# A streaming encoder trunk: joins and closing additions of the last MLP halves by VectorE in place of accumulating DMA

## The chip, the cores and the metric

The kernel runs on one core of a Trainium2 chip. A core has TensorE for matmuls (PE in the profile), VectorE (DVE), ScalarE (ACT), GpSimd (POOL) and SyncE (SP), each with an in-order queue of its own, and 16 DMA engines. The metric is the device time of one execution in microseconds (us); what counts is the median of several runs. Line numbers (L564) are those of the kernel before. In the changed kernel everything below L564 stands four lines lower.

## The reference

The input is 256 tokens by 2048 channels in float32. Two layers are computed, the first with a convolution module as token mixer, the second with latent attention; each is followed by an MLP, and one norm ends the whole:

```python
for layer in range(DEPTH):
    h = rms_norm(x, norm_mixer_g[layer])
    x = x + (conv_module(h, ...) if layer % 2 == 0 else mla(h, ...))
    h = rms_norm(x, norm_mlp_g[layer])
    x = x + jnp.square(jax.nn.relu(h @ mlp_w1[layer])) @ mlp_w2[layer]
return rms_norm(x, final_norm_g)
```

The change concerns the last line in the loop: the product of a 256 x 8192 matrix with the 8192 x 2048 weights mlp_w2, and its addition to the residual x.

## The kernel before

**Arithmetic.** The residual lies in SBUF as one tile, xs, of 128 partitions x 2 token blocks (t) x 2048 columns, in float32. A float32 weight matrix comes in 1 MB pieces (raw, three buffers). Each piece is split into an upper part hi by ScalarE (L169, or L487 in the mixed form) and the rest lo by VectorE (L173, or L488); hi and lo have six buffers each (WB = 6), one half of a piece in each. A product is then three matmuls, hi x hi, hi x lo and lo x hi (mm3, L202 to L204).

**The MLP.** It runs in two halves of the 8192 inner channels (hf = 0, 1). In a half, the first product fills the inner activations, eight groups of 512 channels, and the second product adds the half's share to xs. The second product goes over the output columns in pairs of 512-column blocks, n = 0 and n = 2, so xs is touched by two pairs in each half. Within a pair an object of the class Sums holds eight PSUM banks. Part of the channel groups are *plain*: four banks e collect them directly, one bank per token block and column block. The others are *mixed*: seven products in place of eight on quarter matrices, formed from sums of weights (L495 to L497, VectorE) and of activations; four further banks, u1, u6, u7 and u5, collect some of the seven, the rest go into the banks e. So a unit of two channel blocks of 128 (a *quad* where it is mixed) costs VectorE two 1024-column splits if it is plain, and seven instructions if it is mixed. In the last half there are three mixed groups (layer 0 and layer 1: `MIXED[layer, 1] = (0, 2, 4)`) and five plain ones. For n = 0 units of the two kinds alternate. For n = 2 the last half uses product_A, whose plain pieces have four channel blocks of one column block; mixed quads are put between them in the numbers 1, 2, 1, 2 (the function `between`), and the block n = 3 follows, with plain groups only.

**Joins and closing additions.** When all mixed quads of a pair are done, `join` (L566) turns u1, u6, u7 and u5 into four sums: ScalarE copies u1 into a tile a (L570), VectorE adds the others (L571 to L574), and each of the four results, in SBUF tiles v, goes to its place in xs by `put` (L563): a DMA of 128 x 512 float32 that adds to its destination, issued by GpSimd (L564). When the plain units are done too, `close` (L578) adds the banks e: those of the first column block by VectorE directly (L584), those of the second by a ScalarE copy into a tile v (L587) and another accumulating DMA. The last half of a layer calls join for n = 0 and n = 2 and close for n = 0 only; the banks e of n = 2 and 3 are added by product_A's `add` on VectorE (L377).

**Who reads xs next.** In the last half each finished block is prepared for the following norm (`prepare`): ScalarE squares it and sums the squares (L400, reading xs), and in layer 0 TensorE turns it (L266). In layer 1 VectorE multiplies it by the final gain (L1787).

**The order.** Outside the parts under `manual_schedule` a scheduler sets each engine's order when the kernel is built, and a wait is placed wherever an instruction reads or writes what another one has touched. An instruction that waits holds up all that stands behind it in its engine's queue.

Of the kernel before, what the change touches and what calls it, by code (L numbers as in the profile page):

```python
# [15 lines left out]
ALU = mybir.AluOpType  # L16
# [9 lines left out]
NNB = D // NB  # L26
# [52 lines left out]
def trunk_kernel(  # L79
# [26 lines left out]
    nc = tc.nc  # L106
# [37 lines left out]
    def acc_tile():  # L144
        return psum["acc"].tile([P, NB], F32, tag="acc", name=nm("acc"))
# [375 lines left out]
    class Sums:  # L521


        def __init__(self, n):
            self.n = n
            ps = [acc_tile() for _ in range(8)]
            e, self.u = (ps[:4], ps[4:])[:: 1 if n == 0 else -1]
            self.e = [e[2 * t : 2 * t + 2] for t in range(T)]
            self.begun = set()
# [31 lines left out]
            return xs[:, t, (self.n + c) * NB : (self.n + c + 1) * NB]  # L561

        def put(self, t, c, o):  # L563
            nc.gpsimd.dma_start(self.place(t, c), o, accum_op=ALU.add)  # L564

        def join(self, room):  # L566

            u1, u6, u7, u5 = self.u
            a, b, c, d = (room() for _ in range(4))
            nc.scalar.activation(a, u1, AF.Copy)  # L570
            nc.vector.tensor_tensor(b, u6, a, op=ALU.add)  # L571
            nc.vector.tensor_tensor(c, u7, b, op=ALU.add)
            nc.vector.tensor_tensor(d, u5, c, op=ALU.add)
            nc.vector.tensor_tensor(b, u5, b, op=ALU.add)  # L574
            for (t, n), o in (((0, 0), a), ((1, 0), c), ((1, 1), d), ((0, 1), b)):
                self.put(t, n, o)

        def close(self, room):  # L578

            for c in range(2):  # L580
                for t in range(T):
                    e, x = self.e[t][c], self.place(t, c)
                    if c == 0:
                        nc.vector.tensor_tensor(x, e, x, op=ALU.add)  # L584
                    else:
                        o = room()
                        nc.scalar.activation(o, e, AF.Copy)  # L587
                        self.put(t, c, o)

    def mlp(layer, ssq, next_gain, finish=None, before=None, beside=None, after_up=None):  # L590

        with ExitStack() as cx:
# [22 lines left out]
            for hf in range(HALVES):  # L615
                last = hf == HALVES - 1
# [3 lines left out]
                for g in range(ng):  # L620
# [26 lines left out]
                    for b2 in range(2):  # L647
                        v = v_tile()
                        for b in range(2):
                            o = ps[2 * b2 + b]  # L650
# [18 lines left out]
                def mixed_quad(sums, i):  # L669
                    g, b = ms[i]  # L670
                    sums.mixed(w, k_lo + 4 * g + 2 * b, gs[g][0][:, b], gs[g][1][:, b], i == len(ms) - 1)

                for n in range(0, NNB - 2 * last, 2):
                    sums = Sums(n)
                    ks = [4 * g + 2 * b for g in plain for b in range(2)]
                    at, head = 0, HEAD[n // 2]
                    for i, k in enumerate(ks):
                        upto = -(-len(ms) * (i - head + 1) // (len(ks) - head - TAIL + 1))
                        while at < min(upto, len(ms)):
                            mixed_quad(sums, at)  # L680
                            at += 1
                        if i == len(ks) - TAIL + 1:
                            sums.join(room)
                        sums.plain(w, k_lo + k, hi, lo, k, i == len(ks) - 1)
                    sums.close(room)
                    if last:
                        due += [n, n + 1]
                if last:
                    sums = Sums(NNB - 2)
                    n2 = NNB - 2  # L690

                    def between(n, u, due):
                        if n == n2 and u < len(plain) - 1:
                            for i in range(*(len(ms) * max(i, 0) // (len(plain) - 1) for i in (u, u + 1))):
                                mixed_quad(sums, i)
                        if n == n2 and u == len(plain) - 1:
                            sums.join(room)

                    if after_up is not None:
                        after_up()  # L700
                    product_A(
                        w, k_lo, nkh, hi, lo, add, prepare, range(n2, NNB), due,
                        finish=(lambda t: finish(nssq, t)) if finish is not None else None,
                        before=lambda: before(nssq),
                        groups=plain, banks={n2 + c: [sums.e[t][c] for t in range(T)] for c in range(2)},
                        begun=sums.begun, beside=between,
                    )
# [3 lines left out]
    with ExitStack() as cx:  # L711
# [235 lines left out]
        with tc.manual_schedule():  # L947
# [100 lines left out]
            upper_x, lower_x, last = ((0, 0),), ((0, 1),), ((1, 0),)  # L1048
# [48 lines left out]
            for c in range(1, KC + 1):  # L1097
                n = UC * c
# [6 lines left out]
                if c == KC:  # L1105
# [8 lines left out]
                    c = KC - 1  # L1114
# [105 lines left out]
            for m in range(NP):  # L1220
# [25 lines left out]
                for q in {NP - 3: (0, 1, 4), NP - 2: (5, 2, 3), NP - 1: (6, 7)}.get(m, ()):  # L1246
                    t, i = divmod(q, NNB)
# [13 lines left out]
    def rotary_tables(pool):  # L1261
# [54 lines left out]
        nc.scalar.activation(cos, an2, AF.Sin)  # L1316

    ssq = mlp(0, ssq, g_mix[1], beside=rotary_tables)
    repool("a", acc=6, tr=2)


    with ExitStack() as cx:
# [321 lines left out]
        with tc.manual_schedule():  # L1644
# [87 lines left out]
            for g in range(NG):  # L1732
                for i in range(HG):
                    h = g * HG + i

                    n = -(-len(work) // (HG - i))
# [41 lines left out]
    with ExitStack():  # L1778
# [10 lines left out]
        def finish(ssq, t):  # L1789

            n = NNB - 1
            if t == T - 1:

                nc.vector.tensor_scalar(
                    part[t], ssq[:, t, n : n + 1], scalar1=1.0 / D, scalar2=part[t], op0=ALU.mult, op1=ALU.add
                )
                n += 1
            v = small.tile([P, 1], F32, tag="msf", name=nm("ms"))
            w = small.tile([P, 1], F32, tag="wsf", name=nm("ws"))
            y = small.tile([P, 1], F32, tag="ysf", name=nm("ys"))  # L1800
            q = small.tile([P, 1], F32, tag="qsf", name=nm("qs"))
            nc.scalar.activation(w, ssq[:, t, n : n + 1], AF.Sqrt, scale=1.0 / D, bias=part[t])
            nc.vector.tensor_scalar(v, ssq[:, t, n : n + 1], scalar1=1.0 / D, scalar2=part[t], op0=ALU.mult, op1=ALU.add)
            refined(w, v, y, q)

            stores = []
            cuts = [0, NB // 2, NB, 2 * NB, 3 * NB, D]
            for i, (c0, c1) in enumerate(zip(cuts, cuts[1:])):
                ob = xs[:, t, c0:c1]
                if c1 == D:  # L1810
                    nc.vector.scalar_tensor_tensor(
                        out=ob, in0=ob, scalar=y, in1=gfs[0][:, c0:c1], op0=ALU.mult, op1=ALU.mult
                    )
                elif i in (1, 3):
                    nc.scalar.activation(ob, ob, AF.Copy, scale=y)
                else:
                    nc.vector.tensor_scalar(ob, ob, scalar1=y, scalar2=None, op0=ALU.mult)
                dst = out[0, t * P : (t + 1) * P, c0:c1]
                if i in (1, 3) and t == T - 1:
                    stores.append((dst, ob))  # L1820
                else:
                    nc.sync.dma_start(dst, ob)

            for dst, ob in stores:
                nc.scalar.dma_start(dst, ob)
# [3 lines left out]
        def before(ssq):  # L1829

            for t in range(T):
                m = small.tile([P, 1], F32, tag="msp", name=nm("msp"))
                nc.vector.tensor_reduce(m, ssq[:, t, : NNB - 1], axis=AX.X, op=ALU.add)
                nc.vector.tensor_scalar(m, m, scalar1=1.0 / D, scalar2=EPS, op0=ALU.mult, op1=ALU.add)
                part.append(m)
                for n in range(NNB - 1):
                    gained(t, n)

        mlp(1, ssq, None, finish, before, after_up=load_gf)


# [24 lines left out]
```

## Time and profile before

| what | value |
|---|---|
| median of 3 runs | 1954.84 us (1952.97 to 1958.66) |
| the profiled execution | 1957.43 us, its span 1954.8 us |
| TensorE matmuls / VectorE / ScalarE / GpSimd busy | 99% / 80% / 55% / 13% of the span |
| accumulating DMAs of L564 | 44, each 256 KB |
| granted TensorE clock, mean | 0.999 |
| last half of layer 0: its first pair ends, its second pair's join | about 902 us, about 960 us |
| last half of layer 1: its first pair ends, its second pair's join | about 1857 us, about 1915 us |

The span is the profiled execution from its first to its last instruction; the time around it is a little longer. Views of the trace: the *waits* give who waited for whom, in us in total, number of times and longest; the *stretches* give for each window its length, the engine's busy time, in brackets the number of instructions, the granted clock (1.00 is full), the share of the DMA engines in use and GB/s; the *timeline* gives start, duration, engine, line, operation, written and read tiles, and in square brackets the idle time before the instruction and what ended it.

### The profile page before, as it was taken

The page shows a single profiled execution, that of the slowest core. Times are in us where ns is not written, and L with a number is a line of the kernel's source. Part 1 is how long each engine was busy: PE and PEld are TensorE (multiplying, and loading weights), DVE is VectorE, ACT ScalarE, POOL GpSimd, SP SyncE. Part 2 cuts the span into 40 slices and gives each one's busy share as a digit, 9 for nine tenths or more (in the row PEclk, how much of TensorE's full clock was granted, in tenths as well). Part 3 has the DMA queues.
Part 4 walks back from the last instruction along what each step waited for, and adds up shares of the span by engine and source line. Part 5 has one row for each costly group of instructions (what it writes and reads, how often), then busy time and mean ns, then how long its engine had stood idle before and what let it go on. Part 6 is the DMA issues. An engine that isn't in the chain of part 4 may idle for free.

```text
span 1954.8 us, 28567 instructions
## 1 busy us (share of the span) xinstructions
PE 1929.8 (99%) x10823; PEld 1688.8 (86%) x10823; DVE 1557.0 (80%) x2404; ACT 1084.2 (55%) x1616; POOL 259.2 (13%) x216
## 2 busy tenths in 40 slices
PE   9999999999999999999999999999999999999998
PEld 8999888888888888887789998888888888888876
DVE  7999988877999677697866766877789976777886
ACT  5667755554555455454566565555555655555554
POOL 6999100000010000001001310000000010000000
PEclk9999999999999999999999999999999999999999
DMA  7665556664586766467765445466647686665755
GB/s 232 208 193 174 169 180 212 194 187 158 194 250 227 236 191 194 151 215 205 220 194 146 135 138 192 157 210 194 192 153 232 212 277 188 190 193 194 232 170 169
DMA packets 222569, 379.15 MB, mean 194 GB/s; under 512 B 16216, under 2 KB 91232, under 8 KB 222176
## 3 DMA queue, kind: packets, MB, share of 16 engines
q1 hardware_dynamic: 214768, 363.28, 58.6%
q0 software_dynamic: 6336, 11.54, 3.3%
q10 hardware_dynamic: 1328, 2.52, 0.4%
q8 instruction: 84, 1.38, 0.3%
q14 instruction: 53, 0.43, 0.1%
HBM read 363.68 MB, written 2.10 MB: 187 GB/s over the span
## 4 chain that ended last, share of the span: by engine, by line
issue 25%; PE 19%; DVE 2%; DMA 2%; ACT 1%; POOL 1%; DVEq 0%; ACTq 0%; POOLq 0%
PE acc L633 6%; PE acc L634 3%; PE acc L204 3%; PE acc L202 3%; PE acc L203 3%; DMA xs<-v 2%; DVE lo L488 1%; POOL xs L564 1%; DVE lo L173 1%; DVE raw L495 0%; DMA raw<-in_mlp_w 0%; PE acc L1623 0%; ACT hi L487 0%; ACT hi L169 0%; PE tr L1614 0%
## 5 line engine op out<-in xcount | busy, mean ns | idle before, releaser
L173 DVE TENSOR_TENSOR lo<-raw,hi 128x1024 fp32r<-128x1024 f32 (+2 forms) x519 | 618.9, 1206 | 282.7 <-ACT hi L169 275.6
L169 ACT ACTIVATE hi<-raw 128x1024 fp32r<-128x1024 f32 (+2 forms) x584 | 596.8, 1039 | 397.4 <-PE acc L633 216.3
L633 PE MATMUL acc<-xt,hi 128*128 128x512 f32 x2048 | 710.5, 391 | 0.0
L634 PE MATMUL acc<-xt,lo 128*128 128x256 f32 x2048 | 577.9, 282 | 0.0
L633 PEld LDWEIGHTS acc<-xt,hi 128*128 128x128 f32 x2048 | 384.5, 188 | 79.5
L634 PEld LDWEIGHTS acc<-xt,lo 128*128 128x128 f32 x2048 | 388.1, 189 | 0.2
L487 ACT ACTIVATE hi<-raw 128x1024 fp32r<-128x1024 f32 x224 | 206.6, 948 | 201.0 <-DVE raw L495 118.4
L488 DVE TENSOR_TENSOR lo<-raw,hi 128x1024 fp32r<-128x1024 f32 x224 | 239.0, 1088 | 27.5 <-ACT hi L487 23.3
L564 POOL DMA_DIRECT2D xs<-v x44 | 38.6, 958 | 1501.2 <-DVE lo L173 702.7
L204 PE MATMUL acc<-lo,sh 128*128 128x512 f32 (+1 forms) x524 | 204.4, 390 | 3.9 <-DVE lo L488 3.9
L202 PE MATMUL acc<-hi,sh 128*128 128x512 f32 (+1 forms) x524 | 203.9, 389 | 1.3 <-ACT hi L487 1.2
L204 PE MATMUL acc<-lo,gh 128*128 128x512 f32 x512 | 199.8, 390 | 2.0 <-DVE lo L173 2.0
L202 PE MATMUL acc<-hi,gh 128*128 128x512 f32 x512 | 199.9, 391 | 0.7 <-ACT hi L169 0.6
L203 PE MATMUL acc<-hi,gl 128*128 128x512 f32 x512 | 199.5, 390 | 0.0
L776 PE MATMUL acc<-xt,hi 128*128 128x256 f32 x1024 | 180.2, 281 | 0.4 <-ACT xt L1042 0.3
L203 PE MATMUL acc<-hi,sl 128*128 128x512 f32 (+1 forms) x460 | 178.4, 388 | 0.0
L863 DVE SCALAR_TENSOR_TENSOR sum<-ub,w_dw,sum 128x256 f32<-128x256 f32 x409 | 164.5, 486 | 3.6 <-ACT sum L833 3.0
L173 POOL TENSOR_TENSOR lo<-raw,hi 128x1024 fp32r<-128x1024 f32 x65 | 154.9, 2406 | 17.3 <-ACT hi L169 17.3
L776 PEld LDWEIGHTS acc<-xt,hi 128*128 128x128 f32 x1024 | 154.9, 188 | 1.1 <-ACT xt L1042 0.8
L776 PE MATMUL acc<-xt,lo 128*128 128x256 f32 x512 | 139.4, 280 | 0.0
L204 PEld LDWEIGHTS acc<-lo,sh 128*128 128x128 f32 x524 | 98.4, 188 | 27.8 <-DVE lo L488 8.0
L202 PEld LDWEIGHTS acc<-hi,sh 128*128 128x128 f32 x524 | 98.5, 188 | 22.7 <-ACT hi L487 2.8
(306 smaller groups left out, 2533.8 us busy)
## 6 DMA issues: line engine op xcount, KB each, us to landing
raw<-in_mlp_w SPq DMA_DIRECT2D x256, 1024.0 KB, 5.6
raw<-in_conv_w_pw SPq DMA_DIRECT2D x62, 512.0 KB, 5.2
raw<-in_conv_w_pw SPq DMA_DIRECT2D x16, 1024.0 KB, 5.1
raw<-in_mla_w_o SPq DMA_DIRECT2D x16, 1024.0 KB, 5.6
xs<-v POOLq DMA_DIRECT2D x44, 256.0 KB, 7.6
raw<-in_mla_w_kv_up SPq DMA_DIRECT2D x8, 1024.0 KB, 5.5
raw<-in_mla_w_in SPq DMA_DIRECT2D x8, 576.0 KB, 3.9
raw<-in_mla_w_in SPq DMA_DIRECT2D x4, 1024.0 KB
```

The costliest lines, as they stand in the source:

```text
L169: nc.scalar.activation(hi, raw[:, js, :], AF.Copy)
L173: eng.tensor_tensor(lo, raw, hi.bitcast(F32), op=ALU.subtract)
L202: nc.tensor.matmul(ps, sh, mh, start=start, stop=False)
L203: nc.tensor.matmul(ps, sl, mh, start=False, stop=False)
L204: nc.tensor.matmul(ps, sh, ml, start=False, stop=stop)
L487: nc.scalar.activation(hi, src, AF.Copy)
L488: nc.vector.tensor_tensor(lo, src, hi.bitcast(F32), op=ALU.subtract)
L564: nc.gpsimd.dma_start(self.place(t, c), o, accum_op=ALU.add)
L633: nc.tensor.matmul(ps[b], wh[:, bs], xhl(k), start=k == 0, stop=False)
L634: nc.tensor.matmul(ps[b][:, :S], wl[:, bs], xh(k), start=False, stop=k == KC - 1)
L776: nc.tensor.matmul(pss[c][b][:, :S], w[i][:, bs], (xh, xl)[j](k), start=k == i + j == 0, stop=end and k == k0 + nk - 1 and (i, j) == terms ...
L863: nc.vector.scalar_tensor_tensor(out=out, in0=ubs[c][:, w : w + S], scalar=tap(c, w), in1=base, op0=ALU.mult, op1=ALU.add)
```

## The change

Sums gets a flag, by_dma, that is true in the first half of an MLP (hf = 0) and false in the last one (hf = 1). Where it is false, `put` is a VectorE addition into xs in place of the accumulating DMA; the join's first result is added from its PSUM bank u1, not from the copy a (the copy stays, since the other sums start from it); and `close` adds all four banks e by VectorE, without a ScalarE copy. The first half's calls are as before.

```diff
     class Sums:
-        def __init__(self, n):
-            self.n = n
+        def __init__(self, n, by_dma):
+            self.n, self.by_dma = n, by_dma
...
         def put(self, t, c, o):
-            nc.gpsimd.dma_start(self.place(t, c), o, accum_op=ALU.add)
+            x = self.place(t, c)
+            if self.by_dma:
+                nc.gpsimd.dma_start(x, o, accum_op=ALU.add)
+            else:
+                nc.vector.tensor_tensor(x, o, x, op=ALU.add)
...
             for (t, n), o in (((0, 0), a), ((1, 0), c), ((1, 1), d), ((0, 1), b)):
-                self.put(t, n, o)
+                self.put(t, n, o if self.by_dma or n or t else u1)
...
                     e, x = self.e[t][c], self.place(t, c)
-                    if c == 0:
+                    if c == 0 or not self.by_dma:
                         nc.vector.tensor_tensor(x, e, x, op=ALU.add)
...
                 for n in range(0, NNB - 2 * last, 2):
-                    sums = Sums(n)
+                    sums = Sums(n, not last)
...
                 if last:
-                    sums = Sums(NNB - 2)
+                    sums = Sums(NNB - 2, False)
```

## The prediction

> **What bounds the kernel now.** I read the page first: span, busy times, and the accumulating transfers (each 256 KB, 7.6 us from issue to landing).
>
> ```profile
> span 1954.8 us, 28567 instructions
> ...
> PE 1929.8 (99%) x10823; PEld 1688.8 (86%) x10823; DVE 1557.0 (80%) x2404; ACT 1084.2 (55%) x1616; POOL 259.2 (13%) x216
> ...
> xs<-v POOLq DMA_DIRECT2D x44, 256.0 KB, 7.6
> ```
>
> TensorE is busy for 99% of the span, so a change to the residual additions can be worth only what TensorE stands still because of them. The second view was therefore TensorE's work by stretches: a quiet stretch in a first half, one ahead of a second half's join, then the stretches behind the first pair's end and in the second pair of a last half, layer 0 (900 to 960 us) and layer 1 (1855 to 1942 us).
>
> ```profile
> 530.00:590.00 60.00, 60.00 (x267) 1.00 0.78 237
> 860.00:884.00 24.00, 24.00 (x108) 1.00 0.68 216
> 900.00:932.00 32.00, 29.21 (x121) 1.00 0.48 129
> 1855.00:1887.00 32.00, 28.74 (x119) 1.00 0.52 141
> 965.00:993.00 28.00, 28.00 (x137) 1.00 0.74 212
> ```
>
> The number in brackets counts matmuls. The two quiet rows give one matmul per (60 - 24) / (267 - 108) = 0.226 us, and about 2 more than that for the edges. An unbroken stretch of 32 us would so hold 143. The two behind a pair's end hold 121 and 119: 22 and 24 are missing, **5.0 and 5.4 us of TensorE lost**. The granted clock is 1.00 in all of them, so it isn't throttling. The third view, the waits, says who waits for what there (first row 900 to 960, second 1855 to 1942 on ScalarE; then VectorE 1855 to 1942; then TensorE 900 to 960).
>
> ```profile
> ACT scratch L400 <- DMA xs<-v: 7.6, 2, 4.5
> ACT scratch L400 <- DMA xs<-v: 7.6, 2, 4.6
> DVE xs L377 <- DMA xs<-v: 5.4, 1, 5.4
> PE acc L204 <- DVE lo L488: 2.0, 4, 0.6
> ```
>
> TensorE itself names the weight split (L488), not the transfer; the link is ScalarE's own queue, read in its timeline:
>
> ```profile
> 902.81 1.06 ACT L487 ACTIVATE hi<-raw 128x1024 fp32r<-128x1024 f32 x1
> 908.38 0.63 ACT L400 ACTIVATE scratch<-xs 128x512 f32<-128x512 f32 x1 [4.52 <-DMA xs<-v]
> ...
> 909.01 1.04 ACT L169 ACTIVATE hi<-raw 128x1024 fp32r<-128x1024 f32 x1
> 913.15 0.63 ACT L400 ACTIVATE scratch<-xs 128x512 f32<-128x512 f32 x1 [3.10 <-DMA xs<-v]
> ...
> 913.78 1.04 ACT L169 ACTIVATE hi<-raw 128x1024 fp32r<-128x1024 f32 x1
> ```
>
> The closing sums of the second column block go by ScalarE (L587) and a transfer; the squares for the next norm (L400) wait for it to land, and the splits of the next weights (L169) are queued behind the squares. What VectorE and TensorE make of it:
>
> ```profile
> 910.09 1.23 DVE L173 TENSOR_TENSOR lo<-raw,hi 128x1024 fp32r<-128x1024 f32 x1 [4.96 <-ACT hi L169]
> 914.86 1.23 DVE L173 TENSOR_TENSOR lo<-raw,hi 128x1024 fp32r<-128x1024 f32 x1 [3.54 <-ACT hi L169]
> ...
> 916.14 0.51 PE L204 MATMUL acc<-lo,gh 128*128 128x512 f32 x1 [0.52 <-DVE lo L173]
> ```
>
> At 916 the lead of the splits over TensorE is gone. The four stalls for L488 in the waits above follow in the 16 us behind it and near 956, where two mixed quads in a row keep VectorE busy longer than TensorE. So the transfer's wait is paid as a lost lead, and at several places.
>
> **The change, part by part.** Ten accumulating transfers go in each layer (four per join, twice, and two in the close), two ScalarE copies (L587), and ten VectorE additions come, 20 in all. The order of the changed kernel's instructions shows the rest: TensorE's and SyncE's sequences are unchanged; in ScalarE's the four squares of the first pair follow the additions directly; VectorE has the addition of u1 among the splits before L571, three additions behind L574, and the two closing ones behind L584 and ahead of the next L488. Some splits change place by one or two instructions. GpSimd loses twenty issues and has only small clears behind them; nobody waits for those.
>
> *Removed: the wait behind the first pair.* The price of an addition, VectorE's pause behind them, and the matmul with which the next pair begins:
>
> ```profile
> 898.29 0.69 DVE L584 TENSOR_TENSOR xs<-acc,xs 128x512 f32<-128x512 f32 x1
> 898.90 0.68 DVE L497 TENSOR_TENSOR raw<-raw 128x512 f32<-128x512 f32 x1
> 899.49 0.69 DVE L584 TENSOR_TENSOR xs<-acc,xs 128x512 f32<-128x512 f32 x1
> 902.47 1.23 DVE L488 TENSOR_TENSOR lo<-raw,hi 128x1024 fp32r<-128x1024 f32 x1 [2.28 <-ACT hi L487]
> ```
>
> ```profile
> 901.66 0.39 PE L202 MATMUL acc<-hi,gh 128*128 128x512 f32 x1
> ```
>
> Additions follow each other at 0.60 us, from TensorE's banks or from SBUF. The pair's last matmuls end where the next pair begins, 901.66 plus some 0.3. The closing additions then stand at about 900.5 and 902.0 and end by 902.6, in the 2.28 us in which VectorE waits now: they cost the next split 0.1 us. ScalarE ends its split at 903.9 at the latest (902.81 + 1.06; the two copies L587 ahead of it are gone), then come two squares of some 0.7 us, and the L169 that begins at 909.01 begins by 905.4. The second, which begins at 913.78, needs a buffer again: six are kept, so it waits for the new pair's second half-tile. A half-tile is 12 matmuls, two of them end 24 x 0.226 us behind 901.66, about 907.1 with the last one's run. It begins there, **6.7 us earlier**. VectorE works almost without a pause from 914.86 on, so its row of splits moves forward by 6.7 as well, while TensorE, without its 5.0, moves forward by 5.0. The lead after the first double quad is read here:
>
> ```profile
> 930.63 2.35 DVE L173 TENSOR_TENSOR lo<-raw,hi 128x1024 fp32r<-128x1024 f32 x2
> ```
>
> ```profile
> 932.26 0.39 PE L204 MATMUL acc<-lo,gh 128*128 128x512 f32 x1
> ...
> 956.73 0.50 PE L204 MATMUL acc<-lo,sh 128*128 128x512 f32 x1 [0.49 <-DVE lo L488]
> ```
>
> Now the first of the two L173 ends at 931.8, 0.5 us ahead of TensorE. Afterwards it is 0.5 + 6.7 - 5.0 = 2.2 us ahead. From there to 956.7 VectorE loses its 0.5 and another 0.5, 1.0 us together. With 2.2 at the start that stall goes too, with 1.2 to spare. Saved: 5.0 + 0.5 in layer 0, and 5.4 + 0.5 in layer 1, whose second pair has the same instructions (I take the same 0.5).
>
> *Removed: the wait behind the second pair.* In layer 0 the addition L377 waits as well, but the row 965 to 993 above has TensorE without a gap: worth nothing. In layer 1 it is:
>
> ```profile
> 1925.96 0.69 DVE L377 TENSOR_TENSOR xs<-acc,xs 128x512 f32<-128x512 f32 x1 [5.39 <-DMA xs<-v]
> 1926.57 1.22 DVE L173 TENSOR_TENSOR lo<-raw,hi 128x1024 fp32r<-128x1024 f32 x1
> ```
>
> ```profile
> 1927.84 0.50 PE L204 MATMUL acc<-lo,gh 128*128 128x512 f32 x1 [0.90 <-DVE lo L173]
> ```
>
> The split would start after four more additions (2.4 us) instead of 5.4 us of waiting, 3 us earlier, so its 1.22 us end about 1924.8, and TensorE asks for it at 1927.84 - 0.90 = 1926.9. Saved: 0.9 us. What is late next there is TensorE alone, up to the last addition; the tail behind it doesn't change.
>
> *Added: the joins on VectorE.* Four additions are 2.4 us in each of four places, and behind them stand the splits, for which TensorE waits if the lead is smaller. The first pair's join:
>
> ```profile
> 893.35 1.22 DVE L173 TENSOR_TENSOR lo<-raw,hi 128x1024 fp32r<-128x1024 f32 x1
> ```
>
> This split ends at 894.57. It is the second half-tile of the next pair, and its lower half is read by the 15th matmul, 14 x 0.226 behind 901.66, at 904.8: a lead of 10.3 us against 2.4. In the second pair the addition of u1 comes behind two of the three splits that begin at 956.59:
>
> ```profile
> 956.59 3.49 DVE L173 TENSOR_TENSOR lo<-raw,hi 128x1024 fp32r<-128x1024 f32 x3
> ```
>
> ```profile
> 963.66 0.39 PE L204 MATMUL acc<-lo,gh 128*128 128x512 f32 x1
> ```
>
> The third ends at 960.08, 3.6 us ahead of its first use, against 0.6 us; the other three additions come when plain groups, light on VectorE, have widened the lead. Cost nothing, bounded above by 2.4 in each place, 9.6 in all, if no lead were there; below nothing there is no gain in an addition, and what the missing 20 transfers leave free on the DMA queues I take as nothing, since no stretch with a stall names a weight load.
>
> *The sum.* 5.0 + 0.5 + 5.4 + 0.5 + 0.9 = 12.3 us. The profiled execution took 1957.43 us around its span of 1954.8; it would take 1945.1. The runs shown have the median 1954.84, 2.6 lower; 1954.84 - 12.3 = **1942.5 us**.
>
> *A page against it.* The transfers land in 7.6 us at the median. The Trainium skill, "DMA: Bandwidth & Descriptors", section "Anatomy of one DMA — SWDGE (gpsimd) path", gives such a transfer about 2.0 us and its bytes at 436 GB/s, an estimate of 2.6 us for 256 KB. By that the waits of 4.5 and 5.4 would shrink to nothing and the change would save nothing, 1954.8 us. The trace disagrees with that estimate here: the waits are in it, 4.52 and 3.10 us, so this way gets no chance of its own.
>
> **The rivals.**
>
> *Half of it stays.* The later stalls name L488, VectorE's work for mixed quads. If that load alone makes them, only the stalls next to the waits go, 0.5 us per layer (the row at 916.14) and the 0.9 at the end, 1.9 in all, and the four closing additions (2.4 us) fall into that tight stretch: 1955.3. Between this and the forecast lies 1949, if about half of the lead comes back. Against it: the same quads run in the first halves and up to 900 us without one stall (267 matmuls in 60 us).
>
> *Slower: the joins eat the lead.* If VectorE's additions delay the splits one for one, 20 x 0.60 = 12.0 us fall on TensorE, with 1.9 saved: 1954.84 + 10.1 = 1965. It decides where the lead at the join is below 2.4 us. For it speaks that VectorE is busy for 80% of the span. Against it: 10.3 us of lead at that point, 3.6 at the other against 0.6.
>
> *It doesn't remove the wait.* The squares might wait as long for the closing additions: 1954.8. Against it: those depend on matmuls that end by 902, not on a landing at 908 and 913.
>
> **How the numbers follow.** Forecast 0.75 (1940 to 1945); half of it stays 0.13 (1947 to 1955); slower 0.07 (1957 to 1965); no wait removed 0.05. This kernel's measurement can tell about 0.3%, 5.9 us, from no change. Faster by more: 0.75 and 0.04 of the half case, 0.79; slower by more 0.07; within 0.14. The range reaches from 1939 (the lowest run, 1952.97, less 12.3 and some 1.5 us for the restart behind each stall that the three bracketed terms leave out, and for counts that are off by a matmul) to 1949, the middle of the half case. Outside stay the slower case, the unremoved wait and most of the half case.
>
> **What would show it.** In the changed profile no row with xs<-v may appear between the first pair's end and the next join, and L400 must wait for an L584 addition by a few tenths. The 32 us behind the pair's end should count about 143 matmuls, and the 0.5 us stall in the second pair be gone. If TensorE still waits for L488 at 20 us behind the pair's end, the lead was not restored, and the half case holds; if new waits for L173 stand behind the L568 additions (the new line of the VectorE put), the slower one does.

## The result, and the profile after

The changed kernel takes **1944.19 us** at the median (1943.26 to 1945.93), the kernel before, beside it, 1956.03 us: a ratio of 0.9941 (95% interval 0.9923 to 0.9959), 11.8 us less. Later, beside other runs, it was 0.9942 (0.9930 to 0.9955). The forecast was 1942.5 us, or 12.3 us less.

The page of the changed kernel: the same matmuls, 20 more instructions on VectorE, 20 accumulating transfers fewer, and the span shorter by 10.6 us.

```profile
span 1944.2 us, 28513 instructions
...
PE 1925.7 (99%) x10823; PEld 1688.9 (87%) x10823; DVE 1567.5 (81%) x2424; ACT 1084.0 (56%) x1612; POOL 241.9 (12%) x196
...
xs<-v POOLq DMA_DIRECT2D x24, 256.0 KB, 7.7
```

TensorE's work by stretches in the changed kernel (columns as in the prediction), a quiet stretch first, then those behind the first pair's end in both layers:

```profile
530.00:590.00 60.00, 60.00 (x267) 1.00 0.78 235
...
900.00:932.00 32.00, 32.00 (x143) 1.00 0.48 162
932.00:960.00 28.00, 28.00 (x125) 1.00 0.63 206
1850.00:1882.00 32.00, 32.00 (x143) 1.00 0.49 161
1882.00:1910.00 28.00, 28.00 (x125) 1.00 0.64 211
```

Where 121 and 119 matmuls stood, there are 143, and busy time fills each stretch. TensorE waits for nobody between 900 and 960, nor between 1840 and 1937. ScalarE's waits from 900 to 960 in the changed kernel, and its timeline behind the first pair:

```profile
ACT scratch L400 <- DVE xs L588: 2.7, 2, 2.2
```

```profile
902.05 2.01 ACT L487 ACTIVATE hi<-raw 128x1024 fp32r<-128x1024 f32 x2
903.97 0.61 ACT L400 ACTIVATE scratch<-xs 128x512 f32<-128x512 f32 x1
...
904.71 0.64 ACT L400 ACTIVATE scratch<-xs 128x512 f32<-128x512 f32 x1
...
905.45 1.06 ACT L169 ACTIVATE hi<-raw 128x1024 fp32r<-128x1024 f32 x1
908.17 1.06 ACT L169 ACTIVATE hi<-raw 128x1024 fp32r<-128x1024 f32 x1 [1.66 <-PE acc L203]
```

The squares (L400) of the second block no longer wait for a transfer, and the splits (L169) that stood at 909.01 and 913.78 stand at 905.45 and 908.17, although everything in this execution runs 1.1 us later than in the one of before. That shift is seen in the first closing addition, which also shows where the time came from. The first fence is of the kernel before, the second of the changed one: the first closing addition in layer 0 is already quoted for before (898.29); here are the last but one addition L377 of layer 0 and the first closing addition of layer 1.

```profile
992.61 0.69 DVE L377 TENSOR_TENSOR xs<-acc,xs 128x512 f32<-128x512 f32 x1 [0.79 <-PE acc L204]
...
1853.25 0.68 DVE L584 TENSOR_TENSOR xs<-acc,xs 128x512 f32<-128x512 f32 x1
```

```profile
899.40 0.68 DVE L588 TENSOR_TENSOR xs<-acc,xs 128x512 f32<-128x512 f32 x1
...
987.92 0.69 DVE L377 TENSOR_TENSOR xs<-acc,xs 128x512 f32<-128x512 f32 x1 [0.79 <-PE acc L204]
...
1849.68 0.68 DVE L588 TENSOR_TENSOR xs<-acc,xs 128x512 f32<-128x512 f32 x1
```

Layer 0: 992.61 - 898.29 = 94.3 us before, 987.92 - 899.40 = 88.5 after: 5.8 saved. Layer 1, to the end of the span: 1954.8 - 1853.25 = 101.55 before, 1944.2 - 1849.68 = 94.5 after: 7.0 saved. Together **12.8 us**, all in the two last halves. The spans differ by 10.6, so 2.2 us are lost outside these stretches: 1.1 ahead of the first closing addition (another execution of the changed kernel, after_again below, loses 0.2 there), and 1.1 between the two layers, where a dip of the clock alone costs 1.7 (last section).

### The profile page after: what moved, and what is told of

The parts are those of the page before. It is cut to its first block, busy times and chain, and to the rows that moved or that the text cites. A ratio compares the mean times of both kernels' runs of the same rounds, so it can differ in the third digit from the quotient of the medians.

```text
span 1944.2 us, 28513 instructions
## 1 busy us (share of the span) xinstructions
PE 1925.7 (99%) x10823; PEld 1688.9 (87%) x10823; DVE 1567.5 (81%) x2424; ACT 1084.0 (56%) x1612; POOL 241.9 (12%) x196
## 5 line engine op out<-in xcount | busy, mean ns | idle before, releaser
L173 DVE TENSOR_TENSOR lo<-raw,hi 128x1024 fp32r<-128x1024 f32 (+2 forms) x519 | 618.3, 1205 | 274.6 <-ACT hi L169 271.0
L169 ACT ACTIVATE hi<-raw 128x1024 fp32r<-128x1024 f32 (+2 forms) x584 | 597.5, 1039 | 401.9 <-PE acc L637 214.5
L487 ACT ACTIVATE hi<-raw 128x1024 fp32r<-128x1024 f32 x224 | 206.9, 949 | 202.9 <-DVE raw L495 114.6
L488 DVE TENSOR_TENSOR lo<-raw,hi 128x1024 fp32r<-128x1024 f32 x224 | 238.7, 1087 | 25.2 <-ACT hi L487 20.8
L173 POOL TENSOR_TENSOR lo<-raw,hi 128x1024 fp32r<-128x1024 f32 x65 | 155.1, 2415 | 18.2 <-ACT hi L169 18.2
L566 POOL DMA_DIRECT2D xs<-v x24 | 21.1, 973 | 883.5 <-DVE lo L173 701.6
```

The source lines that it names most:

```text
L169: nc.scalar.activation(hi, raw[:, js, :], AF.Copy)
L173: eng.tensor_tensor(lo, raw, hi.bitcast(F32), op=ALU.subtract)
L487: nc.scalar.activation(hi, src, AF.Copy)
L488: nc.vector.tensor_tensor(lo, src, hi.bitcast(F32), op=ALU.subtract)
L566: nc.gpsimd.dma_start(x, o, accum_op=ALU.add)
```

## The experiments

Theory 1 in the first four runs (close_only, joins_only, late_squares, all_vector) is the prediction's: the close's transfers make the squares wait, the squares hold up ScalarE's splits, and the lost lead is paid as stalls. In the runs after those, Theory 2 is the one that the first four led to: a close's transfer is not issued until the join's transfer into the same place has landed. "Stalls" are TensorE's waits in the last halves. In summary, each beside the kernel before in its own set (medians 1954.34, 1955.73 and 1955.25 us):

| run | what goes by VectorE in the last halves | us, median (lowest to highest) | ratio (95% interval) |
|---|---|---|---|
| close_only | closing additions | 1946.79 (1945.64 to 1949.01) | 0.9962 (0.9949 to 0.9974) |
| joins_only | joins | 1943.49 (1943.32 to 1945.25) | 0.9946 (0.9932 to 0.9960) |
| late_squares | nothing; squares later | 1967.1 (1966.81 to 1968.54) | 1.0066 (1.0053 to 1.0078) |
| all_vector | both, and in the first halves too | 1947.9 (1946.52 to 1948.04) | 0.9965 (0.9952 to 0.9977) |
| half_join | joins into the second column block | 1954.17 (1952.24 to 1956.07) | 0.9988 (0.9979 to 0.9998) |
| other_half | joins into the first column block | 1943.65 (1943.38 to 1944.56) | 0.9934 (0.9919 to 0.9949) |
| late_squares2 | nothing; squares later | 1944.12 (1943.98 to 1944.90) | 0.9937 (0.9922 to 0.9951) |
| pad_shift | nothing; 8 bytes of padding | 1972.82 (1971.5 to 1977.07) | 1.0090 (1.0069 to 1.0110) |
| after_again | the changed kernel | 1943.63 (1943.41 to 1945.92) | 0.9942 (0.9930 to 0.9955) |
| load6 | the same, 6 operations more | 1946.48 (1945.87 to 1946.92) | 0.9953 (0.9939 to 0.9966) |
| load16 | the same, 16 operations more | 1955.17 (1952.83 to 1956.63) | 0.9999 (0.9990 to 1.0008) |
| load8_second | the same, 8 more in the second pair | 1952.72 (1950.69 to 1953.66) | 0.9984 (0.9975 to 0.9993) |

### One part alone

**close_only.** The closing additions by VectorE, all joins by DMA as before. Against the changed kernel:

```diff
-            if self.by_dma:
+            if True:
                 nc.gpsimd.dma_start(x, o, accum_op=ALU.add)
...
-                self.put(t, n, o if self.by_dma or n or t else u1)
+                self.put(t, n, o)
```

> Only the closing additions of the last halves go to VectorE; all joins stay accumulating transfers (40 of 44 remain). Theory 1 (ScalarE's queue waits for the close's transfers, and the lost lead is paid as stalls): the 22 and 24 matmuls missing in the 32 us behind the first pair's end come back, the stall of 0.5 us in the second pair goes, only the 0.9 us at the end stays; 1944 to 1946, about 11 us faster than before. Theory 2 (the transfers cost by their number, through traffic or their queue): 4 of 20 removed, some 2.4 us faster. Theory 3 (the gain is in the joins): no change.

It was 1946.79 us, 7.5 us less than the kernel before, where about 11 were expected. Behind the first pair there are no stalls (143 matmuls from 900 to 932, and from 1850 to 1882). Measured by stretches as above, 11.3 of the 12.8 us are saved. What is left is a wait at the end of layer 1; TensorE's timeline of close_only, and VectorE's at the close in layer 0:

```profile
1917.98 0.51 PE L204 MATMUL acc<-lo,gh 128*128 128x512 f32 x1 [0.77 <-DVE lo L173]
```

```profile
903.80 0.69 DVE L588 TENSOR_TENSOR xs<-acc,xs 128x512 f32<-128x512 f32 x1 [3.24 <-DMA xs<-v]
```

So the tail's wait is still there where the second pair's join goes by DMA, as the prediction had it; late_squares2 below shows that the join's transfers alone do not suffice for it. The second line says something new: the closing addition itself has to wait, 3.2 us, for a transfer of the join into the same place. The addition, unlike a transfer, is then done in 0.7 us.

**joins_only.** The joins by VectorE, the close as before (a ScalarE copy and a transfer):

```diff
-                    if c == 0 or not self.by_dma:
+                    if c == 0:
                         nc.vector.tensor_tensor(x, e, x, op=ALU.add)
...
-                        self.put(t, c, o)
+                        nc.gpsimd.dma_start(x, o, accum_op=ALU.add)
```

> Only the joins of the last halves go to VectorE; the second column block is closed by ScalarE copies and accumulating transfers as before (28 of 44 remain). Theory 1: the stalls behind the first pair's end stay (about 120 of 143 matmuls in 32 us) and only the 0.9 us at the end go; 0 to 2 us faster than before. Theory 2 (by number): 16 of 20 removed, 9 to 10 us faster. Theory 3 (joins): all of it, 12 us faster.

Measured: 1943.49 us, and not one stall. Theory 1 said that these four transfers, which all stay, make the wait; it is refuted in that form. Their issue on GpSimd first in the kernel before, then in joins_only:

```profile
893.24 1.75 POOL L564 DMA_DIRECT2D xs<-v  x2 [1.90 <-DVE v L573]
904.33 1.75 POOL L564 DMA_DIRECT2D xs<-v  x2 [9.34 <-ACT hi L487]
```

```profile
902.03 0.87 POOL L592 DMA_DIRECT2D xs<-v  x1 [252.12 <-ACT v L591]
903.46 0.86 POOL L592 DMA_DIRECT2D xs<-v  x1 [0.56 <-ACT v L591]
```

In the kernel before, both copies L587 are done by 902.9, and yet the issue comes at 904.33; the profile names ScalarE's L487, which has nothing to do with these tiles. The instruction list of the built program says more. These are the last two transfers of the join and the two of the close on GpSimd, with what they wait for; a semaphore counts 16 for each landing:

```
L564 DMACopy xs<-v_8880 128x512 [waits DMASW6>=16, DVE]         its landing: DMASW6 = 32
L564 DMACopy xs<-v_8878 128x512 [waits DMASW7>=16, DVE]         its landing: DMASW7 = 32
L564 DMACopy xs<-v_8926 128x512 [waits DMASW7>=32, Activation]
L564 DMACopy xs<-v_8929 128x512 [waits DMASW6>=32, Activation]
```

Both pairs add into the same two places of xs, and the program holds the close's pair back until the join's has landed. In the trace the later one of the join's lands at 903.70, and the close's issue follows 0.6 us behind it. And once issued, the close's pair is slower. The median from issue to landing, of the join's last two and of the close's two in the kernel before, and of the close's two in joins_only:

```profile
xs<-v POOLq DMA_DIRECT2D x2, 256.0 KB, 7.8
```

```profile
xs<-v POOLq DMA_DIRECT2D x2, 256.0 KB, 6.1
```

```profile
xs<-v POOLq DMA_DIRECT2D x2, 256.0 KB, 3.2
```

In joins_only the two go out singly, 1.4 us apart, as their copies are ready; each lands in 3.2 us, and the squares wait 1.3 us for one of them. In the kernel before they go out together, about 0.6 us apart: the first lands in 4.0 us and the second in 8.1 (the squares that wait for them begin at 908.38 and 913.15, as the prediction shows). All of the join's transfers had landed by then. In every pair that goes out together here the second is the slower one; why is not shown. ScalarE in joins_only:

```profile
905.30 0.63 ACT L400 ACTIVATE scratch<-xs 128x512 f32<-128x512 f32 x1 [1.29 <-DMA xs<-v]
...
905.93 1.04 ACT L169 ACTIVATE hi<-raw 128x1024 fp32r<-128x1024 f32 x1
```

### Which of the join's transfers

**half_join and other_half.** Two of the join's four results go by VectorE, two by DMA, and the close goes by DMA. half_join (other_half has `c == 1`), the close as in joins_only; in half_join the first result, which goes by a transfer again, comes from the copy a:

```diff
-            if self.by_dma:
+            if self.by_dma or c == 0:
                 nc.gpsimd.dma_start(x, o, accum_op=ALU.add)
```

> In the last halves only the two join results that go into the second column block (the places into which the close's two transfers of the first pair are added next) go by VectorE; the two of the first column block stay transfers, and so does the close: 16 of the 20 transfers' partners stay in order, 32 to 36 accumulating transfers are left. Theory 2 (a close's transfer waits for the join's transfer into the same place, so that two run in series): the close's transfers are issued within 1 us of their copies, ScalarE's L400 waits under 2 us, the stalls behind the first pair go in both layers, 10 to 11.5 us: 1943 to 1945.5 if before is at 1954.8. Theory 1 (the close's transfers make the wait by themselves): no gain there, 1953 to 1955. By their number (every transfer less helps alike): 8 of 20 transfers gone, 4 to 5 us: 1950.

> The mirror of the run above: the two join results into the first column block go by VectorE, the two into the second stay transfers, and the close stays as before. Theory 2: the close's transfers still wait for the join's into the same place; the join's two may land somewhat earlier because two fewer are ahead of them, so 0 to 4 us less than before: 1951 to 1955. By their number: as in the run above, 4 to 5 us: 1950. If this run gains as much as the one above, theory 2 falls.

The outcome is the reverse of what Theory 2 expected: half_join gains 1.6 us, other_half all of it. By its own words, Theory 2 falls as the full answer. Yet in both runs the stalls right behind the first pair are gone and the squares wait 1.3 us for a transfer. GpSimd in other_half:

```profile
890.99 1.76 POOL L566 DMA_DIRECT2D xs<-v  x2 [242.30 <-DVE v L577]
902.33 0.86 POOL L592 DMA_DIRECT2D xs<-v  x1 [9.57 <-ACT v L591]
```

Here the join's transfers into the close's places are still there. But they are issued at 890.99, not at 893.24, and have landed (a median of 7.4 us) when the copy is ready, so the close's issue waits for the copy alone. The order costs only where the join's transfer lands late. Here it lands 4 us sooner: 2.3 us come from the issue, since VectorE has its additions and splits in another order in this program, and the rest from a quicker landing. Whether two transfers fewer make that difference, or the order, these runs do not tell apart. What Theory 2 kept of the mechanism stands; that the place alone decides does not.

half_join loses elsewhere, in the second pair. A stall of 0.5 us for L488 stays in each layer, and the transfers into the first column block hold up L377, as they did before, but now TensorE loses 3.0 us by it and not 0.9 (VectorE, then TensorE, layer 1):

```profile
1919.25 0.69 DVE L377 TENSOR_TENSOR xs<-acc,xs 128x512 f32<-128x512 f32 x1 [4.49 <-DMA xs<-v]
```

```profile
1921.13 0.51 PE L204 MATMUL acc<-lo,gh 128*128 128x512 f32 x1 [2.99 <-DVE lo L173]
```

The same happens in layer 0 (1.8 us at 967.44). Over the two last halves, measured as above, half_join saves 4.3 + 2.65 = 6.95 us of the 12.8; the second number already holds a dip of the clock behind the wait of 3.0 us. The spans differ by 2.5 us. Of the 4.5 lost outside these stretches a second dip, behind the end of layer 0, takes about 1.7; the rest is not explained. The medians differ by 1.6 us (0.4 to 4.1).

### ScalarE's queue by itself

**late_squares.** The kernel before with all its 44 transfers; only the squares of the first pair's second block are made to stand later in ScalarE's queue, by a bias column of zeros that VectorE writes behind the second double quad of the next pair:

```diff
+                        bias = held["zero"] if n == 1 and "zero" in held else 0.0
-                        nc.scalar.activation(out, xs[:, t, sl], AF.Square, accum_out=ssq[:, t, i : i + 1])
+                        nc.scalar.activation(out, xs[:, t, sl], AF.Square, bias=bias, accum_out=ssq[:, t, i : i + 1])
...
+                held["quads"] += 1
+                if held["quads"] == 2:
+                    held["zero"] = small.tile([P, 1], F32, tag="late", name=nm("late"))
+                    nc.vector.tensor_scalar(
+                        held["zero"], t1[1][:, 0:1].bitcast(F32), scalar1=0.0, scalar2=None, op0=ALU.mult
+                    )
```

> The kernel before with all 44 accumulating transfers; only the squares of the first pair's second column block are made to wait for a weight split in the second pair (a zero bias column taken from that split), so that they stand behind the landing in ScalarE's queue. Theory 1: TensorE's stalls behind the first pair's end go although no transfer is removed, 143 matmuls in 32 us, 9 to 11.5 us faster than before; the 0.9 us at the end stays. Theory 2: no transfer removed, no change.

It came out 12.8 us slower, and not through the squares: stretches far from them are slower too. From 530 to 590 us late_squares has 259 matmuls, with no wait of TensorE:

```profile
530.00:590.00 60.00, 60.00 (x259) 1.00 0.76 228
```

The new tile had moved the tiles allocated behind it. So the experiment was run again without that, and a move was run alone.

**late_squares2** takes the column from a tile that the kernel has already; **pad_shift** is the kernel before with a padding tile that is 8 bytes longer:

```diff
-                    held["zero"] = small.tile([P, 1], F32, tag="late", name=nm("late"))
+                    held["zero"] = small.tile([P, 1], F32, tag="warm", name=nm("late"))
```

```diff
-PAD_SMALL = 48
+PAD_SMALL = 50
```

> Before, with all 44 accumulating transfers, but the squares of the first pair's second block take a zero column that VectorE writes behind the second double quad of the next pair, so that ScalarE's queue runs the splits ahead of them. The zero column lies in a tile that the kernel had already, so that no other tile changes place. If the loss is ScalarE's queue standing behind the squares (both theories): 9 to 11 us less than before, 1944 to 1946, with 143 matmuls in the 32 us behind the first pair. If the transfers themselves disturb TensorE or the weight loads: 1953 to 1956.

> Before, with the padding tile of the pool of small tiles two columns (8 bytes) longer and nothing else changed: a control for the run late_squares, whose new tile of 8 bytes shifted every tile allocated behind it. If the slower matmuls there (0.232 us instead of 0.227 apart in the stretches of the second product, at a granted clock of 1.00) came from the shifted places: about 10 to 20 us slower than before, 1965 to 1975, with the same 259 matmuls from 530 to 590 us. If they came from the late squares: no change, 1953 to 1957, 267 matmuls.

late_squares2: 1944.12 us, as good as the changed kernel, with all 44 transfers. In the built program TensorE, GpSimd and SyncE have the same instructions in the same order as before, and in ScalarE's order only these squares have moved. The stretch behind the first pair, and ScalarE there:

```profile
900.00:932.00 32.00, 32.00 (x143) 1.00 0.63 195
```

```profile
904.63 1.06 ACT L169 ACTIVATE hi<-raw 128x1024 fp32r<-128x1024 f32 x1 [0.48 <-PE acc L203]
907.35 1.06 ACT L169 ACTIVATE hi<-raw 128x1024 fp32r<-128x1024 f32 x1 [1.66 <-PE acc L203]
916.75 0.73 ACT L401 ACTIVATE scratch<-xs,late 128x512 f32<-128x512 f32 x1 [0.41 <-DVE late L546]
```

The transfers still land late; nobody minds, since the splits stand ahead of the squares. This shows the core of the prediction by itself: the stalls were ScalarE's queue standing behind the squares, and the transfers cost TensorE nothing. Not even the wait at the end of layer 1 is left, although VectorE waits there for a transfer of the second pair's join as before:

```profile
1913.11 0.69 DVE L377 TENSOR_TENSOR xs<-acc,xs 128x512 f32<-128x512 f32 x1 [5.19 <-DMA xs<-v]
```

The split behind this addition still ends before TensorE needs it.

pad_shift: 17 us slower than before, the same 259 matmuls. The rows behind the first pairs follow:

```profile
530.00:590.00 60.00, 60.00 (x259) 1.00 0.75 227
...
909.00:941.00 32.00, 31.35 (x134) 1.00 0.54 159
1870.00:1902.00 32.00, 29.75 (x123) 1.00 0.47 127
```

Against this control, late_squares gains: the ratios 1.0066 and 1.0090 are 4.7 us apart. It has 139 matmuls in each of the two lower stretches, so pad_shift misses 5 and 16 there, 21 x 0.232 = 4.9 us. That is all there is to win: before, 46 were missing. The slower TensorE probably leaves the splits more time.

### How much VectorE can take

**all_vector.** VectorE in the first halves as well, with no accumulating transfer left:

```diff
-                    sums = Sums(n, not last)
+                    sums = Sums(n, False)
```

> The changed kernel with VectorE in the first halves too, no accumulating transfer left. Theory 1: the first halves have no wait for a transfer in ScalarE's queue and no stall, so the time is that of the changed kernel, 1943 to 1946; new stalls only if VectorE's lead in the first halves is below 2.4 us. Theory 2 (by number): 24 more transfers gone, a further 14 us faster.

1947.9 us, above the 1943 to 1946 expected and 4.4 us above joins_only in the same set. There are new stalls in the first halves, in layer 1 for example:

```profile
1522.70 0.50 PE L202 MATMUL acc<-hi,sh 128*128 128x512 f32 x1 [0.57 <-ACT hi L487]
1524.11 0.50 PE L204 MATMUL acc<-lo,sh 128*128 128x512 f32 x1 [0.69 <-DVE lo L488]
```

TensorE had no stall in the first halves before, so there was nothing to win, and the additions cost lead: in the 200 us around these places 7 and 8 matmuls are missing against the changed kernel.

**load6, load16, load8_second.** The changed kernel with 6 or 16 idle VectorE operations behind the first pair's join, or 8 behind the second pair's (`self.n` in place of `self.n == 0`), beside **after_again**, which is the changed kernel:

```diff
+            for _ in range(6 if self.n == 0 and not self.by_dma else 0):
+                nc.vector.tensor_tensor(a, a, a, op=ALU.max)
```

> The changed kernel once more, beside the runs below and in more rounds. Both theories: 1943 to 1946, 10 to 12 us less than before. Its first profile lost 1.7 us from 994 to 998 us at a granted clock of 0.57, behind a wait of TensorE of 2 us; if that is an accident of one execution, the median is about 1943, as in the runs other_half, late_squares2 and joins_only; if it belongs to the kernel, about 1944.5.

> The changed kernel with six more VectorE operations (128x512, on a scratch tile, results unused) behind the first pair's join of each last half, 6 x 0.60 = 3.6 us per layer, standing between the splits as the planner puts them. The lead theory: VectorE's own pauses from 899 to 910 us are 3.1 us (0.31 + 0.67 + 0.63 + 1.49), and the lead after that is 1 to 2 us, so it costs 0 to 1.5 us in all: at most 1946 where the changed kernel is at 1944. The theory that VectorE's additions fall on TensorE one for one: 7.2 us more, 1951.

> As load6, with sixteen operations, 9.6 us per layer. The lead theory: 9.6 less 3.1 of pauses less 1 to 2 of lead leaves 4.5 to 5.5 us per layer, 9 to 11 in all, 1953 to 1955, with stalls for L488 and L173 behind the first pair as in the kernel before. One for one: 19 us more, 1963. If nothing appears, the lead is far larger than I worked out.

> The changed kernel with eight such operations at the second pair's join of each last half, 4.8 us per layer; three of them or so stand ahead of the splits that TensorE needs next, the others between later ones. The prediction's margin there was 3.6 us less one addition of 0.6: 3.0. The lead theory: 0 to 2 us per layer, up to 1948 where the changed kernel is at 1944, with a wait for L173 near 963 and 1920 us if any. One for one: 9.6 us more, 1953.5.

Against after_again's 1943.63 us: load6 +2.9 us for 7.2 us of work, where 0 to 1.5 were expected; load16 +11.5 for 19.2, just above the top of the 9 to 11 expected; load8_second +9.1 for 9.6, where 0 to 4 were expected. So the lead theory came out too low three times. Of load6's loss TensorE's waits show 0.8 us; where the rest goes is open. TensorE's stretches in load16, and its longest wait in total:

```profile
900.00:932.00 32.00, 30.48 (x130) 1.00 0.41 133
1850.00:1882.00 32.00, 29.18 (x125) 1.00 0.48 154
1882.00:1910.00 28.00, 26.80 (x115) 1.00 0.57 189
```

```profile
PE acc L202 <- ACT hi L487: 4.9, 6, 1.5
```

These are 13, 18 and 10 matmuls fewer than in the changed kernel, 41 x 0.226 = 9.3 us, about as many as the transfers' wait had cost. Here VectorE alone makes them, without any transfer: TensorE waits for ScalarE's L487, which waits for the sums that VectorE forms (L495, L497), and only 0.4 us for L488. load8_second has its stall in one piece, at the end of layer 1 (TensorE's waits from 1905 to 1930, and its stretch from 1916):

```profile
PE acc L204 <- DVE lo L173: 4.5, 1, 4.5
```

```profile
1916.00:1924.00 8.00, 4.42 (x10) 0.63 0.16 44
```

In layer 0 it has none. In layer 1 the scheduler put seven of the eight operations, with the final norm's own VectorE work, ahead of the split that TensorE needed next. Much of the rest of the 9.1 us is the clock, which stood at 0.63 over these 8 us: (1 - 0.63) x 8 = 3.0. The total is near that of the one-for-one theory, 9.6, but by chance: the wait and the dip are in layer 1 alone, and a third is the clock's.

No version beats the others: the changed kernel, joins_only, other_half and late_squares2 lie between 1943.5 and 1944.2 us, with no stall left in the last halves that any of them could take away.

## Why the prediction was right

- **The wait behind the first pair, 5.0 + 5.4 us: right.** 22 and 24 missing matmuls are back. The splits were forecast by 905.4 and at 907.1; with the execution's shift of 1.1 us that is 906.5 and 908.2, and they stand at 905.45 and 908.17.
- **The lead and the second pair's 0.5 us each: right.** Forecast was a lead of 2.2 us behind the first double quad. VectorE's pair of splits there and TensorE's first use, in the changed kernel:

```profile
925.28 2.35 DVE L173 TENSOR_TENSOR lo<-raw,hi 128x1024 fp32r<-128x1024 f32 x2
```

```profile
928.37 0.39 PE L204 MATMUL acc<-lo,gh 128*128 128x512 f32 x1
```

  The first of the two ends near 926.5: 1.9 us ahead. The stall that stood at 956.73 is gone.
- **The tail, 0.9 us: right for this change.** close_only, which keeps the join's transfers, keeps the wait (0.8 us). But late_squares2 keeps them too and has none, so it takes the transfers and a small lead together.
- **The joins on VectorE at nothing: right for these twenty additions.** TensorE waits for nobody while they run. VectorE's additions of the first pair in the changed kernel:

```profile
891.58 1.88 DVE L568 TENSOR_TENSOR xs<-v,xs 128x512 f32<-128x512 f32 x3
...
901.60 0.69 DVE L588 TENSOR_TENSOR xs<-acc,xs 128x512 f32<-128x512 f32 x1 [0.31 <-PE acc L204]
902.96 0.69 DVE L588 TENSOR_TENSOR xs<-acc,xs 128x512 f32<-128x512 f32 x1 [0.67 <-PE acc L204]
```

  But the reason given, a lead of 10.3 us against 2.4, was too generous. load6 puts 3.6 us more there and has its first new wait (0.8 us for L173, in layer 1's second pair); load16, with 9.6 us more, has the full stalls. The margin that counts is over all that follows, VectorE's pauses and the lead behind them. The runs bound it only from above: less than 3.6 us per layer, since load6 already costs time. The rival "the joins eat the lead" names a real mechanism, and the change stays a few us short of it.
- **The freed DMA queues at nothing: right.** late_squares2 has all 44 transfers and the same time. The reason given, that no stretch with a stall names a weight load, was too wide: from 1855 to 1942 ScalarE's splits do wait 8.5 us for weight loads in the kernel before. TensorE does not wait for them there.
- **Who makes the wait: incomplete.** The prediction put it down to the close's transfers. The runs show a chain: the join's transfers land late, the close's wait for them and then land in 6.1 us at the median, not 3.2. Cutting it at the join or at ScalarE's queue gives the full gain, cutting it at the close 7.5 us of it by the medians. So the shares were wrong, 11.4 us for the close and 0.9 for the join: alone they gain 7.5 and 10.9, which do not add up. The sum was right because the change cuts the chain twice, whichever link is the cause. A forecast for joins_only by the same step would have been wrong by some 10 us, and was.
- **The page against it.** By the Trainium skill, "DMA: Bandwidth & Descriptors", section "Anatomy of one DMA — SWDGE (gpsimd) path", such a transfer was estimated at 2.6 us. The close's two in joins_only take 3.2, near it; in the kernel before the medians are 6.1 to 7.8, and the prediction was right to go by them. But it was wrong that the waits would shrink to nothing at 2.6 us: with the issue at 904.33 the first landing would be at 906.9, still 3 us after ScalarE had ended its split at 903.9. The late issue, more than the slow landing, made the first wait.
- **The size.** 12.3 us were forecast, 12.8 are found in the two last halves, and the medians differ by 11.8 and 11.6. In the profiled execution about 1.7 us went to the clock.

## What to carry to other kernels

Where TensorE waits in small pieces for an engine that is not full, look for the one long wait in some queue ahead of it; the stalls are that wait, paid later. Then ask what the long wait itself waits for: here the program issues an accumulating transfer only when the one before it into the same place has landed, and taking the first one away, or moving the waiter behind the urgent work, was enough. Additions moved to VectorE are free only within its pauses and its lead over the next few steps, which a few idle operations added at the spot measure directly.

## What the runs showed of the hardware

**A shift in the places of the tiles** slows the matmuls of these stretches from 267 to 259 in 60 us at a granted clock of 1.00: 17 us over the kernel. late_squares and pad_shift, whose edits have nothing else in common, show the same count. In the built programs the tiles lie at multiples of 32 bytes, so the 8 bytes more in pad_shift move the tiles behind them by 32, and the new tile of late_squares moves them by 64. pad_shift's instructions and their order are those of the kernel before. Its pieces of the weights (raw, hi, lo), its xs and its PSUM banks lie where they lay, and its activations (gh, gl, sh, sl), the other operand of these matmuls, have moved. Why that makes a matmul slower is open. A new small tile is thus no neutral edit here.

**A dip of the clock behind a wait of 2 us.** The profiles have this wait of TensorE at the end of layer 0, here from the changed kernel's:

```profile
PE acc L202 <- DVE xt L215: 2.0, 1, 2.0
```

Behind it, TensorE from 993 to 998 us in the changed kernel, and in joins_only, whose wait ends within a us of the same time:

```profile
993.00:998.00 5.00, 5.00 (x26) 0.66 0.03 12
```

```profile
993.00:998.00 5.00, 5.00 (x40) 1.00 0.00 0
```

The clock stood at half for some 3.4 us of these 5, which loses (1 - 0.66) x 5 = 1.7 us. Both profiles of the changed kernel, close_only, half_join and the three load runs have the dip; the kernel before, joins_only, other_half, both late_squares runs, pad_shift and all_vector have the same wait and no dip. It does not seem to belong to a kernel: of the changed kernel's nine executions four have a mean clock of 0.998 and take 1945.1 to 1945.9 us, both profiled ones among them, and five have 0.999 and take 1943.3 to 1943.6. Where in an execution the clock fell, the mean does not say. The dip accounts for most of what separates their spans (1943.3 us for after_again, 1941.7 for joins_only). The Trainium skill, "TensorE: Matmul & The Clock Gate", Part 1, gives a free-running window of about 3.4 us and half speed behind an idle one; the half and the length agree with these rows. But that page names gaps over about 3.4 us as those that bring it on, and here one of 2.0 us was enough in some executions. What decides between them stays open.
